# An encoder block on one core: the token tiles' transpositions a turn later, two weight splits behind the second chunk's numerators, and the last chunk and the last part's first token in another order

## The chip, the cores and the metric

The kernel runs on one core of one Trainium2 chip. The metric is the device time of one execution in microseconds (us). Before the change it is 2493.55, the median of three runs (2489.95 to 2499.76).

## The reference

Input `x` has 2048 tokens of 1024 values; one layer of an encoder is computed in fp32:

```python
xn = rmsnorm(x, norm_mix)
q, k, v, o, g = split(xn @ w_in)        # 4 heads, keys of 128, values of 256, gates g
h_fwd = mlstm_scan(q, k, v, g[0], g[1])                      # chunks of 128 tokens
h_bwd = flip(mlstm_scan(flip(q), flip(k), flip(v), g[2], g[3]))
h = head_norm(h_fwd + h_bwd) * sigmoid(o)
h1 = x + h @ w_out
h2 = h1 + square(relu(rmsnorm(h1, norm_mlp) @ w1)) @ w2      # 1024 -> 4096 -> 1024
gate = sigmoid(rmsnorm(h2, norm_ple) @ gate_w + gate_b)
out = rmsnorm(h2 + gate * (p @ ple_w), norm_final)           # p: 256 values per token
```

In each chunk the scan makes scores `q k^T`, weighs them with exponentials, multiplies them with `v` (the numerators), adds the carried state's share `q C`, divides by a denominator that comes out of the same product, and updates the state `C` for the next chunk.

## The kernel before, in words

Every large fp32 product is made of three matmuls: each operand is split into a high part (`hi`, a cast on ScalarE, ACT in the profile) and the remainder (`lo`, a subtraction on VectorE, DVE), and `mm3` multiplies hi·hi, hi·lo and lo·hi into one PSUM tile. Line 100 is the wrapper through which VectorE, ScalarE and TensorE instructions are recorded, so most rows of the profile carry it; the tile's name tells what a row is.

The program has four parts. First the input projections with the backward scan. Then the forward scan with the output projection, in 16 chunks (class `Chunk`, line 683), some 25 us each. Then the MLP, whose products are made by a seven-product scheme on 2x2 blocks (`run7`, line 1111) and whose down products end at about 2236 us. Then the last part (class `Tok`, line 1216): for 16 tiles of 128 tokens the gate product, the `ple_w` product and the last norm.

A chunk's steps are written as a list of short names that is walked for each turn of the loop over chunks (`step`, line 1375): `n0` and `n1` are the numerators with the forward and the backward state (PSUM tile `pn`, copied by ScalarE to `nt`), `s` the state product (`pu`, then `Cn` and its cast `Chi`), `T` the transpositions of the chunk before (`pth` out of `jk`, then `hThi` and `hTlo`), `S` the scores of the next chunk (`pS`), `e`, `k`, `w`, `q` and `v` its exponentials (`mb`), weighted keys (`wk`), weights (`pTh`), split queries (`qsh`) and split values (`vh`, `vl`), `p` the product of keys and gates of the chunk after next on GpSimd (`ib`, engine POOL), `m` and `me` the norm of the heads (root `rsa`, `rst`, `rsy`, then `jk`), `o0` and `o1` the two halves of the output projection of the chunk before (`pso`, added to the residual `xt`), and `d`, `d1`, `d2` loads. The Tile framework's scheduler takes this program order as priority and sets each engine's order from it, so that instructions of neighbouring steps end up interleaved.

There are three such lists beside the ordinary `ORDER`. `TR` (line 1390) is chunk 0, woven into the last input projections; in it `a0` to `a7` load and `c0` to `c7` split the eight tiles of `w_out` (`wst`, then `whi` and `wlo`). `ORDER_X` (line 1414) is used in turns that also prepare a tile of tokens for the MLP (`Tokens0.steps`, line 1009): `xl` loads 128 rows of the mixer's output (`raw`), `xn` norms them to `xs`, `xt` transposes them (eight matmuls into `pt`, copies to `zt`, one store). These steps begin in turn `XC` = 7 and run through turn 14. `TAIL` (line 1421) is the last chunk, mixed with the preparation of the first MLP product: `W` loads, `P1` and `P2` make its weight operands (`sa` and `op`), `Z`, `U` and `X` its token operands, `T15`, `y0` and `y1` are the last chunk's own transpositions and output projection.

Around the last part the dictionary `late` hangs loads and splits on the last steps of the down products; the two tiles of `ple_w` (`wpl`) are loaded in step 46 and split in step 47, the last. Then the loop over the 16 token tiles calls, for each, `tr0` of the next tile, `half(0)`, `tr1` of the next tile and `half(1)`, where `half` makes 24 matmuls into `pg`, six into `pl`, and the additions, sigmoid and squares behind them.

Of the kernel before, what the change touches and what calls it, by code (L numbers as in the profile page):

```python
# [17 lines left out]
S = 2048  # L18
# [17 lines left out]
def hybrid_mlstm_kernel(  # L36
# [28 lines left out]
    def ps_mm(name):  # L65
        return psm.tile([P, 512], F32, tag="mm", bufs=4, name=name)
# [1149 lines left out]
    class Tok:  # L1216
# [23 lines left out]

        def half(self, n):

            if n == 0:
                self.ss = small("ssf")
            sl = slice(n * 512, (n + 1) * 512)
            pg = ps_mm("pg")
            tk = slice((self.t % 4) * P, (self.t % 4 + 1) * P)
            for k in range(KD):
                mm3(pg, self.hi[:, k], self.lo[:, k], wgt[k].hi[:, sl], wgt[k].lo[:, sl], k == 0, k == KD - 1)
            pl = ps_tr("pl")  # L1250
            for k in range(2):
                mm3(pl, self.pt.hi[:, k, tk], self.pt.lo[:, k, tk], wpl[k].hi[:, sl], wpl[k].lo[:, sl], k == 0, k == 1)
            g, h = St("g", [P, 512]), self.h2[:, sl]
            V.tensor_tensor(g, pg, rowc["gb"][:, sl], op=ALU.add)
            act(g, g, AF.Sigmoid)
            V.tensor_tensor(g, pl, g, op=ALU.mult)
            V.tensor_tensor(h, g, h, op=ALU.add)
            A.activation(g, h, AF.Square, scale=1.0 / 32.0, accum_out=self.ss[:, n:n + 1])
# [116 lines left out]
    def step(c, nm):  # L1375
# [30 lines left out]
    def row_load(nm, src):  # L1406
        rowc[nm] = Ht(f"row_{nm}", [P, D])
        SP.dma_start(rowc[nm], src.partition_broadcast(P))


    XC = 7
    tp = {c: x0.steps(c - XC) for c in range(XC, XC + 8)}
    tp[XC][0] = lambda f=tp[XC][0]: (row_load("mlp", norm_mlp[0]), f())
    ORDER_X = "n0 d1 s e T S n1 d2 k w xl q sl m v d xn o0 o1 xt me p".split()
    for c in range(1, NC - 1):
        for nm in ORDER_X if c in tp else ORDER:
            if nm in ("xl", "xn", "xt"):
                tp[c][("xl", "xn", "xt").index(nm)]()
            else:
                step(c, nm)()  # L1420
    TAIL = "d2 W n1 Z1 Z3 T n0 Z2 Z4 o0 m me P1 X1 T15 P2 o1 U3 U1 y0 X2 U2 X3 y1".split()
    l = ch[NC - 1]
    u0 = up[0][0]
    extra = {"T15": l.transposes, "y0": lambda: l.out(0), "y1": lambda: l.out(1), "W": u0.left.dma,
             "P1": lambda: [f() for f in u0.prep[:3]], "P2": lambda: [f() for f in u0.prep[3:]],
# [44 lines left out]
    for g in range(4):  # L1470
# [6 lines left out]
            45: [wgt[5].prep, wgt[6].dma, wgt[7].dma, pp[0].get, toks[1].norm, toks[3].load],  # L1477
            46: [wgt[6].prep, wgt[7].prep, wpl[0].dma, wpl[1].dma, toks[0].tr0, pp[0].split],
            47: [wpl[0].prep, wpl[1].prep, toks[0].tr1, lambda: row_load("nf", norm_final)]}
    for s, fs in late.items():  # L1480
# [4 lines left out]
    for t in range(NC):  # L1485
        nx = toks[t + 1] if t + 1 < NC else None
        if nx:
            nx.tr0()
        toks[t].half(0)
        if t + 4 < NC:  # L1490
            toks[t + 4].load()
        if nx:
            nx.tr1()
        if t % 4 == 2 and t + 2 < NC:
            pp[t // 4 + 1].split()
        if t % 4 == 0 and t + 4 < NC:
            pp[t // 4 + 1].get()
        toks[t].half(1)
        if t > 0:
# [26 lines left out]
```

## Time and profile before

| | us |
|---|---|
| median of three runs | 2493.55 |
| profiled execution | 2496.48 |
| its span in the trace | 2494.8 |
| turn 1, from 600.32 to 630.05 | 29.73 |
| turn 4, from 679.44 to 702.74 | 23.30 |
| turn 7, from 751.85 to 778.02 | 26.17 |
| turns 8 to 14, from 778.02 to 937.20 | 159.18 |
| turn 15, from 937.20 to 955.90 | 18.70 |
| the last chunk's output projection, to 974.87 | 18.97 |

A turn is counted here from the first numerator matmul of a chunk to that of the next. It contains the end of one pass through the list and the beginning of another, since TensorE's order follows the scheduler. The last part starts at about 2236.5. In the timelines a row gives the start, the duration, the engine, the line, the operation with its output and inputs, how many of them are merged, and in brackets how long the engine had been idle and what released it.

### The profile page before, as it was taken

Reading aid. Unit: us, or ns where it says so; the run is one execution under the profiler, and the core shown is the slowest. Engines: PE = TensorE matmul, PEld = TensorE weight load, DVE = VectorE, ACT = ScalarE, POOL = GpSimd, SP = SyncE. Lnnn points to the kernel's source line nnn. Section 1 sums busy time; section 2 is a strip of 40 time slices with the busy share of each in tenths; the row PEclk is TensorE's granted clock in tenths of the full one; section 3 lists DMA queues with packets and bytes.
Section 4 is the critical chain, followed back from the end, with each engine's and each line's share of the span. In section 5 each row is a group of like instructions: output and inputs, shape, how many; then the busy total and the mean of one; then the engine's idle time right before and its main releaser. Section 6 shows DMA issues by size and latency. Waiting matters only on the chain.

```text
span 2494.8 us, 31616 instructions
## 1 busy us (share of the span) xinstructions
PE 2415.3 (97%) x11413; PEld 1987.1 (80%) x11413; DVE 1525.7 (61%) x2533; ACT 1134.5 (45%) x2134; POOL 610.9 (24%) x609
## 2 busy tenths in 40 slices
PE   7999999998899999999999999999999999999998
PEld 6988898787778887788878888787887888777776
DVE  5152336456787888656775445766676667655665
ACT  5031324336667885443353333444443444445554
POOL 1040022124433334344733333111111111110000
PEclk9999999999999999999999999999999999999999
DMA  7177337867566765455763331467686776882211
GB/s 250 48 207 238 91 101 243 271 216 276 201 210 212 254 234 190 144 169 169 257 203 125 114 112 59 160 146 178 142 185 166 176 173 153 184 219 84 85 54 49
DMA packets 270134, 420.72 MB, mean 169 GB/s; under 512 B 46441, under 2 KB 181993, under 8 KB 269977
## 3 DMA queue, kind: packets, MB, share of 16 engines
q1 hardware_dynamic: 211416, 299.03, 36.7%
q0 software_dynamic: 58272, 119.15, 20.4%
q8 instruction: 89, 1.46, 0.2%
q14 instruction: 69, 0.56, 0.1%
q10 hardware_dynamic: 288, 0.52, 0.1%
HBM read 253.43 MB, written 165.01 MB: 168 GB/s over the span
## 4 chain that ended last, share of the span: by engine, by line
PE 52%; DVE 4%; DMA 3%; ACT 2%; issue 1%; SPq 0%; POOL 0%; ACTq 0%; DVEq 0%
PE pa L100 26%; PE pb L100 13%; PE pc L100 6%; PE pg L100 5%; DMA hst<-hid_d 1%; PE pl L100 1%; DMA wst<-in_mlp_w 1%; DVE op L100 1%; PE pt L100 1%; DVE h L100 1%; DMA z<-tz_d 1%; ACT L100 1%; DVE xs L100 1%; PE pso L100 1%; DVE rst L100 1%
## 5 line engine op out<-in xcount | busy, mean ns | idle before, releaser
L100 PE MATMUL pa<-op 128*128 128x512 f32 x3072 | 753.2, 394 | 7.6 <-ACT e L100 4.1
L100 PEld LDWEIGHTS pa<-op 128*128 128x128 f32 x3072 | 575.4, 188 | 147.6 <-ACT e L100 7.8
L100 PE MATMUL pb<-op 128*128 128x512 f32 x1536 | 384.3, 394 | 1.2 <-DVE op L100 0.8
L100 PEld LDWEIGHTS pb<-op 128*128 128x128 f32 x1536 | 288.1, 188 | 70.0 <-ACT e L100 1.2
L100 PE MATMUL psf<-xT,whi 128*128 128x512 f32 x1024 | 320.8, 394 | 0.0
L100 DVE TENSOR_TENSOR op<-sa,op 128x768 fp32r<-128x768 f32 (+2 forms) x160 | 167.6, 1053 | 137.9 <-ACT op L100 106.1
L1162 POOL DMA_DIRECT2D h_d<-o x96 | 93.1, 977 | 567.8 <-DVE o L100 507.3
L100 PEld LDWEIGHTS psf<-xT,whi 128*128 128x128 f32 x1024 | 191.3, 188 | 43.7
L100 ACT COPY e<-pa 128x512 f32<-128x512 f32 x160 | 93.7, 586 | 261.6 <-PE pa L100 260.9
L100 ACT CAST op<-sa 128x768 fp32r<-128x768 f32 (+2 forms) x160 | 139.6, 879 | 146.7 <-PE pb L100 66.6
L100 PE MATMUL psf<-xT,wlo 128*128 128x512 f32 x512 | 201.8, 394 | 0.0
L100 PE MATMUL pc<-op 128*128 128x512 f32 x768 | 191.6, 394 | 0.2 <-DVE op L100 0.2
L100 PEld LDWEIGHTS pc<-op 128*128 128x128 f32 x768 | 144.1, 188 | 34.1 <-DVE op L100 0.6
L100 PE MATMUL psv<-whi,xT 128*128 128x272 f32 (+2 forms) x720 | 160.9, 317 | 0.6 <-DVE xT L98 0.6
L100 PEld LDWEIGHTS psv<-whi,xT 128*128 128x128 f32 x720 | 118.6, 188 | 9.8 <-DVE xT L98 0.8
L100 DVE TENSOR_TENSOR op<-wst,op 128x512 fp32r<-128x512 f32 x96 | 108.6, 1134 | 28.7 <-ACT op L100 16.0
L884 POOL TENSOR_TENSOR sa<-wst 128x512 f32<-128x512 f32 x32 | 60.4, 1887 | 263.9 <-PE pb L100 167.6
L100 ACT CAST op<-wst 128x512 fp32r<-128x512 f32 x96 | 79.3, 834 | 93.8 <-DVE op L100 59.3
L100 DVE TENSOR_TENSOR wlo<-wst,whi 128x1024 fp32r<-128x1024 f32 (+2 forms) x64 | 77.1, 1214 | 60.4 <-ACT whi L100 49.4
L100 PE MATMUL psv<-wlo,xT 128*128 128x272 f32 (+2 forms) x360 | 114.0, 317 | 0.0
L100 PEld LDWEIGHTS psf<-xT,wlo 128*128 128x128 f32 x512 | 96.1, 188 | 22.4
L100 PE MATMUL pg<-whi,xTl 128*128 128x512 f32 x256 | 102.5, 400 | 0.0
(228 smaller groups left out, 4318.6 us busy)
## 6 DMA issues: line engine op xcount, KB each, us to landing
wst<-in_mlp_w SPq DMA_DIRECT2D x96, 512.0 KB
h_d<-o POOLq DMA_DIRECT2D x96, 512.0 KB, 12.8
hid_d<-e SPq DMA_DIRECT2D x128, 256.0 KB
hst<-hid_d SPq DMA_DIRECT2D x64, 384.0 KB
wst<-in_mlstm_w_in SPq DMA_DIRECT2D x44, 512.0 KB
vst<-v_d SPq DMA_DIRECT2D x31, 512.0 KB
raw<-in_x SPq DMA_DIRECT2D x16, 512.0 KB
kq<-kq_d SPq DMA_DIRECT2D x16, 512.0 KB
```

Source lines behind the costliest of these rows:

```text
L100: r = f(*a, **kw)
L884: eng.tensor_tensor(s[:, 0], r1[:, :, P:], r2[:, :, P:], op=add_)
L1162: G.dma_start(rows(h1_d, 2 * q + i), o[i], accum_op=add_)
```

## The change

There are four edits.

`TR` loses `c6` and `c7`: the splits of the last two `w_out` tiles move into turn 1, behind `T` and behind `k w`, by a list `ORDER_1` of that turn's own.

`XC` becomes 6, so that token tiles are loaded and normed in turns 6 to 13, and `xt` in turn c now transposes the tile that was normed in turn c − 1, behind `n1`, where it stood at the turn's end for the same turn's tile. Transpositions are then in turns 7 to 14.

`TAIL` puts `P1`, `X1`, `o1` and `P2` ahead of the last chunk's transpositions, and its two output halves go behind the first of the seven products of the first MLP job (`u0.post[0]`).

In the last part `half` gives its gate product to a function `gate`. For the first token tile both gate products and both transpositions of the next tile are issued first, then the splits of the two `ple_w` tiles, then the rest of both halves. The `ple_w` loads move from step 46 to step 47.

```diff
-        def half(self, n):
+        def gate(self, n):
+            sl = slice(n * 512, (n + 1) * 512)
+            self.pg = pg = ps_mm("pg")
+            for k in range(KD):
+                mm3(pg, self.hi[:, k], self.lo[:, k], wgt[k].hi[:, sl], wgt[k].lo[:, sl], k == 0, k == KD - 1)
+
+        def half(self, n, gate=True):
...
+            if gate:
+                self.gate(n)
+            sl, pg = slice(n * 512, (n + 1) * 512), self.pg
...
         "D1 a0 D c0 o6a a1 o6b o7a v0 p0 S0 a2 o7b b0 c1 e0 d_ S k0 w0 a3 q0 b1 c2 p_ a4 n0 c3 e s d1 d2 sl k w a5 "
-        "n1 v b2 q m d c4 a6 me b3 c5 p c6 a7 c7").split()
+        "n1 v b2 q m d c4 a6 me b3 c5 p a7").split()
...
-    XC = 7
+    XC = 6
...
-    ORDER_X = "n0 d1 s e T S n1 d2 k w xl q sl m v d xn o0 o1 xt me p".split()
+    ORDER_1 = "n0 d1 s e T c6 S n1 d2 k w c7 q sl m v d o0 o1 me p".split()
+    ORDER_X = "n0 d1 s e T S n1 xt d2 k xl w q sl m v d xn o0 o1 me p".split()
...
-        for nm in ORDER_X if c in tp else ORDER:
+        for nm in ORDER_X if c in tp or c - 1 in tp else ORDER if c > 1 else ORDER_1:
...
-    TAIL = "d2 W n1 Z1 Z3 T n0 Z2 Z4 o0 m me P1 X1 T15 P2 o1 U3 U1 y0 X2 U2 X3 y1".split()
+    TAIL = "d2 W n1 Z1 Z3 T n0 Z2 Z4 o0 m me P1 X1 o1 P2 T15 U3 U1 X2 U2 X3".split()
...
+    u0.post[0][:0] = [lambda: l.out(0), lambda: l.out(1)]
...
-            46: [wgt[6].prep, wgt[7].prep, wpl[0].dma, wpl[1].dma, toks[0].tr0, pp[0].split],
-            47: [wpl[0].prep, wpl[1].prep, toks[0].tr1, lambda: row_load("nf", norm_final)]}
+            46: [wgt[6].prep, wgt[7].prep, toks[0].tr0, pp[0].split],
+            47: [wpl[0].dma, wpl[1].dma, toks[0].tr1, lambda: row_load("nf", norm_final)]}
...
-        toks[t].half(0)
+        if t == 0:
+            toks[t].gate(0)
+            pg0 = toks[t].pg
+            nx.tr1()
+            toks[t].gate(1)
+            pg1 = toks[t].pg
+            wpl[0].prep()
+            wpl[1].prep()
+            toks[t].pg = pg0
+        toks[t].half(0, t > 0)
```

ScalarE's order in turn 1, as one piece of the difference. `mb` are exponentials of the next chunk, `whi` casts of `w_out` tiles, `nt` the copies of numerators, `hThi` the high part of the transposed heads.

```order
 L100 ACTIVATE jk<-nt,rsy 128x256 x3
 L100 CAST whi<-wst 128x1024
-L100 ACTIVATE mb<-mb,gcol 128x128 x6
-L100 CAST whi<-wst 128x1024
-L100 ACTIVATE mb<-mb,gcol 128x128 x2
-L100 CAST whi<-wst 128x1024
+L100 ACTIVATE mb<-mb,gcol 128x128 x3
 L100 COPY nt<-pn 128x257 x4
-L100 CAST Chi<-Cn 128x1032
-L100 CAST hThi<-og 128x512 x2
+L100 ACTIVATE mb<-mb,gcol 128x128 x5
+L100 CAST Chi<-Cn 128x1032
```

Two casts have left the stretch ahead of the four `nt` copies; they stand behind `hThi` and behind the weights `pTh` now.

GpSimd's order in a turn with a token tile, before:

```order
L167 TENSOR_TENSOR qsl<-ib,qsh 128x1024
L641 MEMSET vh 128x4x2
L641 MEMSET vl 128x4x2
L642 MEMSET vh 128x4
L736 AFFINE_SELECT mb<-mb 128x512
L726 TENSOR_TENSOR ib<-kq,ib 128x512 x2
L706 DMA Chi<-cb_d 128x1032
L706 DMA Clo<-cb_d 128x1032
L736 AFFINE_SELECT mb<-mb 128x512
```

and after:

```order
L167 TENSOR_TENSOR qsl<-ib,qsh 128x1024
L641 MEMSET vh 128x4x2
L641 MEMSET vl 128x4x2
L642 MEMSET vh 128x4
L726 TENSOR_TENSOR ib<-kq,ib 128x512 x2
L706 DMA Chi<-cb_d 128x1032
L706 DMA Clo<-cb_d 128x1032
L736 AFFINE_SELECT mb<-mb 128x512 x2
```

Both products `ib` now stand ahead of both selects on `mb`, as they do in turns without a token tile.

ScalarE's order at the first token tile of the last part, before (`e` and `o` are the last results of the down products, `pTh` the high part of the tokens' `p`, `whi` the two `ple_w` tiles):

```order
L100 COPY e<-pb 128x512
L100 CAST xTh<-pt 128x512
L100 CAST pTh<-z 128x1024
L100 CAST whi<-wst 128x1024
L100 CAST xTh<-pt 128x512
L100 CAST whi<-wst 128x1024
L100 COPY o<-pa 128x512
L100 CAST xTh<-pt 128x512
```

and after:

```order
L100 CAST xTh<-pt 128x512
L100 COPY e<-pa 128x512
L100 COPY e<-pb 128x512
L100 CAST pTh<-z 128x1024
L100 CAST xTh<-pt 128x512 x2
L100 CAST whi<-wst 128x1024
L100 COPY o<-pa 128x512
L100 CAST whi<-wst 128x1024
```

Neither `ple_w` cast stands ahead of the two `xTh` casts any more.

## Rows read from the trace of the kernel before

**Rows 1.** The page's first part: busy time, share of the span and instructions of each engine (PEld is TensorE's weight load).

```profile
PE 2415.3 (97%) x11413; PEld 1987.1 (80%) x11413; DVE 1525.7 (61%) x2533; ACT 1134.5 (45%) x2134; POOL 610.9 (24%) x609
```

**Rows 2.** The waits of TensorE over the whole span: what waited for what, total us, times, the longest.

```profile
PE pu L100 <- ACT nt L100: 16.1, 14, 7.4
PE pt L100 <- DVE xs L100: 11.6, 16, 1.4
PE pt L100 <- DVE xTl L100: 5.8, 1, 5.8
PE pth L100 <- ACT jk L100: 3.3, 1, 3.3
```

**Rows 3.** Windows: from and to, length, busy us (instructions) of PE, PEld, DVE, ACT and POOL, granted clock of TensorE, share of the DMA engines, GB/s. In their order here: a low-clock stretch of turn 3, turn 4, turn 7, turns 8 to 14, turn 15, and the low-clock stretches of turn 1, of the last part, of the last chunk and of turn 7.

```profile
661.60:665.00 3.40, 3.39 (x16) 3.39 (x17) 3.37 (x8) 1.15 (x2) 0.42 (x1) 0.50 0.95 294
679.44:702.74 23.30, 21.52 (x126) 18.28 (x124) 17.70 (x35) 16.10 (x45) 8.65 (x11) 1.00 0.65 215
751.85:778.02 26.17, 23.78 (x125) 20.99 (x124) 18.95 (x36) 17.16 (x45) 8.43 (x10) 0.87 0.53 171
778.02:937.20 159.18, 149.92 (x925) 132.14 (x923) 133.38 (x286) 130.01 (x357) 60.09 (x68) 1.00 0.70 244
937.20:955.90 18.70, 17.62 (x101) 15.03 (x100) 12.47 (x24) 13.20 (x34) 5.22 (x3) 1.00 0.83 277
...
610.40:617.20 6.80, 4.72 (x22) 4.73 (x23) 3.31 (x7) 3.36 (x7) 0.00 (x0) 0.50 0.70 243
2238.50:2245.40 6.90, 3.10 (x10) 2.62 (x11) 2.74 (x3) 3.52 (x6) 0.17 (x1) 0.51 0.61 185
958.50:965.40 6.90, 5.43 (x16) 4.10 (x17) 5.41 (x8) 4.74 (x8) 0.28 (x1) 0.51 1.06 375
757.20:764.00 6.80, 6.37 (x29) 6.18 (x29) 3.44 (x8) 4.50 (x13) 2.34 (x4) 0.50 0.80 245
```

**Rows 4.** Timeline of turn 1, around the last cast of a `w_out` tile.

```profile
611.10 1.04 ACT L100 CAST whi<-wst 128x1024 fp32r<-128x1024 f32 x1 [3.92 <-DMA wst<-in_mlstm_w_out]
...
612.05 1.19 ACT L100 COPY nt<-pn 128x257 f32<-128x257 f32 x4
...
612.48 0.58 PE L100 MATMUL pu<-vh,wk 128*128 128x258 f32 x1 [7.38 <-ACT nt L100]
```

**Rows 5.** Timeline of the last chunk, on both sides of the end of chunk 14's output projection.

```profile
950.60 0.68 DVE L100 TENSOR_TENSOR xt<-pso,xt 128x512 f32<-128x512 f32 x1
950.60 1.30 POOL L884 TENSOR_TENSOR sa<-wst 128x512 f32<-128x512 f32 x1 [18.92 <-PE pso L100]
...
958.83 1.71 ACT L100 ACTIVATE jk<-nt,rsy 128x256 f32<-128x256 f32 x4 [4.56 <-DVE rsy L100]
959.39 1.97 PE L100 MATMUL pth<-ident,jk 128*128 128x128 f32 x8 [3.33 <-ACT jk L100]
...
961.94 0.79 PE L100 MATMUL pso<-whi,hThi 128*128 128x512 f32 x1 [0.58 <-ACT hThi L100]
```

**Rows 6.** Timeline of the last part's first token tile.

```profile
2239.34 1.04 ACT L100 CAST whi<-wst 128x1024 fp32r<-128x1024 f32 x1 [6.96 <-DMA wst<-in_ple_w]
...
2242.30 1.11 PE L100 MATMUL pt<-ident,xs 128*128 128x128 f32 x4 [5.76 <-DVE xTl L100]
...
2243.41 1.04 ACT L100 CAST whi<-wst 128x1024 fp32r<-128x1024 f32 x1 [2.54 <-DMA wst<-in_ple_w]
...
2244.49 1.23 DVE L100 TENSOR_TENSOR wlo<-wst,whi 128x1024 fp32r<-128x1024 f32 x1 [2.24 <-ACT whi L100]
...
2246.06 0.39 PE L100 MATMUL pg<-wlo,xTh 128*128 128x512 f32 x1
...
2246.29 0.39 PE L100 MATMUL pg<-whi,xTl 128*128 128x512 f32 x1
```

**Rows 7.** Timeline of turn 10, a turn with a token tile, which starts at 823.45.

```profile
825.91 1.09 PE L100 MATMUL pt<-ident,xs 128*128 128x128 f32 x8 [1.35 <-DVE xs L100]
826.32 2.53 POOL L726 TENSOR_TENSOR ib<-kq,ib 128x512 f32<-128x512 f32 x2
826.37 1.25 DVE L100 TENSOR_TENSOR rsy<-rsy,rst 128x4 f32<-128x4 f32 x1
...
828.77 0.28 PE L100 MATMUL pu<-vh,wk 128*128 128x258 f32 x1
...
838.22 0.32 SPq L696 DMA_DIRECT2D ib<-in_d  x1
```

**Rows 8.** Timeline of turn 4, a turn without a token tile, which starts at 679.44, from the end of the turn before it on.

```profile
677.12 3.59 POOL L726 TENSOR_TENSOR ib<-kq,ib 128x512 f32<-128x512 f32 x2 [1.75 <-DMA ib<-in_d]
677.23 1.23 DVE L100 TENSOR_SCALAR rsa<-ssh 128x4 f32<-128x4 f32 x1
...
679.50 1.24 DVE L100 TENSOR_TENSOR rst<-rsa,rsy 128x4 f32<-128x4 f32 x1
680.77 0.16 DVE L100 TENSOR_TENSOR rst<-rst,rsy 128x4 f32<-128x4 f32 x1
...
681.37 1.71 ACT L100 ACTIVATE jk<-nt,rsy 128x256 f32<-128x256 f32 x4 [2.44 <-DVE rsy L100]
...
684.26 0.39 PE L100 MATMUL pu<-vh,wk 128*128 128x258 f32 x1 [1.28 <-ACT nt L100]
```

**Rows 9.** Timeline of VectorE at the start of turn 2.

```profile
628.97 2.34 DVE L100 TENSOR_TENSOR vl<-vst,vh 128x1024 fp32r<-128x1024 f32 x1 [0.77 <-ACT vh L100]
```

More of the change, by code (lines that the diff above doesn't have):

```diff
@@ L1239, in hybrid_mlstm_kernel @@
         tr0, tr1 = (lambda self: self.tr(0)), (lambda self: self.tr(1))
-        def half(self, n):
+        def gate(self, n):
[4 more added lines that the diff above has]
+        def half(self, n, gate=True):
             if n == 0:
                 self.ss = small("ssf")
-            sl = slice(n * 512, (n + 1) * 512)
-            pg = ps_mm("pg")
+            if gate:
+                self.gate(n)
+            sl, pg = slice(n * 512, (n + 1) * 512), self.pg
             tk = slice((self.t % 4) * P, (self.t % 4 + 1) * P)
-            for k in range(KD):
-                mm3(pg, self.hi[:, k], self.lo[:, k], wgt[k].hi[:, sl], wgt[k].lo[:, sl], k == 0, k == KD - 1)
             pl = ps_tr("pl")
@@ L1408, in row_load @@
         SP.dma_start(rowc[nm], src.partition_broadcast(P))
-    XC = 7
+    XC = 6
     tp = {c: x0.steps(c - XC) for c in range(XC, XC + 8)}
     tp[XC][0] = lambda f=tp[XC][0]: (row_load("mlp", norm_mlp[0]), f())
-    ORDER_X = "n0 d1 s e T S n1 d2 k w xl q sl m v d xn o0 o1 xt me p".split()
+    ORDER_1 = "n0 d1 s e T c6 S n1 d2 k w c7 q sl m v d o0 o1 me p".split()
+    ORDER_X = "n0 d1 s e T S n1 xt d2 k xl w q sl m v d xn o0 o1 me p".split()
     for c in range(1, NC - 1):
-        for nm in ORDER_X if c in tp else ORDER:
-            if nm in ("xl", "xn", "xt"):
-                tp[c][("xl", "xn", "xt").index(nm)]()
+        for nm in ORDER_X if c in tp or c - 1 in tp else ORDER if c > 1 else ORDER_1:
+            if nm == "xt":
+                tp.get(c - 1, [lambda: None] * 3)[2]()
+            elif nm in ("xl", "xn"):
+                tp.get(c, [lambda: None] * 3)[("xl", "xn").index(nm)]()
+            elif nm in ("c6", "c7"):
+                wo[int(nm[1])].prep()
             else:
                 step(c, nm)()
-    TAIL = "d2 W n1 Z1 Z3 T n0 Z2 Z4 o0 m me P1 X1 T15 P2 o1 U3 U1 y0 X2 U2 X3 y1".split()
+    TAIL = "d2 W n1 Z1 Z3 T n0 Z2 Z4 o0 m me P1 X1 o1 P2 T15 U3 U1 X2 U2 X3".split()
     l = ch[NC - 1]
     u0 = up[0][0]
-    extra = {"T15": l.transposes, "y0": lambda: l.out(0), "y1": lambda: l.out(1), "W": u0.left.dma,
+    extra = {"T15": l.transposes, "W": u0.left.dma,
              "P1": lambda: [f() for f in u0.prep[:3]], "P2": lambda: [f() for f in u0.prep[3:]],
@@ L1488, in hybrid_mlstm_kernel @@
             nx.tr0()
-        toks[t].half(0)
+        if t == 0:
[8 more added lines that the diff above has]
+        toks[t].half(0, t > 0)
         if t + 4 < NC:
             toks[t + 4].load()
-        if nx:
+        if nx and t > 0:
             nx.tr1()
@@ L1497, in hybrid_mlstm_kernel @@
             pp[t // 4 + 1].get()
-        toks[t].half(1)
+        if t == 0:
+            toks[t].pg = pg1
+        toks[t].half(1, t > 0)
         if t > 0:
```

## The prediction, before any run of the changed kernel

> **What bounds the kernel now.** I read the busy shares first, then the waits of TensorE, then the windows around the places the diff touches, then their timelines. TensorE is busy for 97% of the span and VectorE, the next, for 61% [rows 1], so time can come only from its idle stretches and from the stretches in which it ran at its lower clock. The list of its waits names the idle ones [rows 2]: 16.1 us before a state product (`pu`) for the copy of a numerator (`nt`), 7.4 of them in one wait; 11.6 us in 16 waits of a token's transposition (`pt`) for its normalized tile (`xs`); one wait of 5.8 for the low half of a transposed token (`xTl`); one of 3.3 for the normalized heads (`jk`). The windows give the clock as granted [rows 3]: 1.00 (2.4 GHz) over turns 8 to 14, 0.50 (1.2 GHz) in short stretches, three of which hold a place the diff edits. A matmul that runs in such a stretch takes twice as long, so half of TensorE's busy time there is lost. I call a chunk's stretch between two starts of its first numerators a turn.
>
> The kernel's own sum is made against the profiled execution, 2496.48 us; the median of the runs shown, 2493.55, is 2.93 lower, and I subtract that at the end. A difference under 0.5% (12.5 us) is about what a measurement of this kernel can't tell from no change.
>
> **Turn 1: the last two w_out splits.** Before, ScalarE stands 3.92 us before the second of the two casts, for a weight's transfer that lands at 611.10, and only then copies four numerators, for which TensorE waits 7.38 us [rows 4]. The low clock holds from 610.40 to 617.20 with 4.72 us of TensorE work in it [rows 3], half of it lost: 2.36. Together 9.7. The changed order puts both casts behind the copies, so this wait goes. What is late next: the four copies with the six or eight small `mb` activations before them, some 1.0 us before `pu`; the `out` product, whose heads come from ScalarE next to a cast of 1.04, some 1.7; the low half of the last tile, some 0.6. 9.7 − 3.3 = 6.4, of which I take **−6.2**, from −8.5 (only the 1.0 is left) to −4 (the low clock stays). These three left-over waits are estimates from the durations in [rows 4].
>
> **Last chunk.** TensorE waits 3.33 us for `jk` and 0.58 for `hThi` [rows 5], and from 958.50 the clock is 0.50 with 5.43 us of work in it, half lost: 2.7 [rows 3]. That is 6.6. Now the first MLP product's twelve matmuls (2.8 us at the full clock) and the numerators' second half are put in front of the transpositions. They cover most of the 3.33, but ScalarE has the casts of that product to do ahead of `jk`, so `jk`, 1.71 long, comes later too; I leave 1.4 for it and 0.9 for `hThi`, whose successor no longer has filler. 6.6 − 2.3 = **−4.3**, from −6 to −2.5.
>
> **First token of the last part.** ScalarE waits 6.96 us for the first of two `ple_w` tiles, in front of the cast that makes `xTh`; so the transposed token is late and TensorE waits 5.76 [rows 6]. The low clock from 2238.50 holds 3.10 us of work, 1.55 lost [rows 3]: 7.3 together. In the changed program the gate products of both halves, 48 matmuls of 0.23 (the step between two of them) [rows 6], with both transpositions, stand ahead of the first use of `ple_w`, which puts that use at about 2247.2. The second tile landed at 2243.41; its cast and subtraction, 1.04 and 1.23 [rows 6], are done by 2245.8. So 1.4 us of cover is left if the transfers, now issued one step later, land as before; landing over 1.4 later, each further us is a us of wait. I take **−6.2**, from −7.3 to −4.5.
>
> **Turns 8 to 14: the transposition.** These take 159.18 us, 22.74 each, with 149.92 of TensorE work, 21.42 each, at clock 1.00 [rows 3]. Of the idle 1.32 a turn nearly all is the transposition's wait for `xs` (1.35 in turn 10 [rows 7]). A turn later that wait goes, since `xs` is then a turn old. But it was not only lost: while TensorE stood there and did the eight transpositions (1.09), ScalarE caught up, and `pu` came with no wait at 828.77 [rows 7]. Without transposition in that place `pu` follows the numerators directly, as in the turns without token work. Turn 4 is the nearest row: 23.30 long with 21.52 of work [rows 3], 1.78 idle, most of it the 1.28 before `pu` [rows 8]. There `jk` (1.71) must pass before the `nt` copies, and `jk` waits 2.44 for the reciprocal root (`rsa`, `rst`, `rsy`: small operations of VectorE).
>
> Why that root is late, the rows show: GpSimd's two `ib` products run from 677.12 for 3.59, and the VectorE operations that start just behind the beginning of one take 1.23 and 1.24 in place of 0.16 [rows 8]. In the changed order of token turns GpSimd's products come before both selects of `mb`, as in turn 4, so they meet the root's operations, unless their data come later or earlier. In turn 10 one such operation met them too (1.25), but behind the wait, where it cost little [rows 7]. The data of `ib` are asked for at 838.22, in the turn before [rows 7], and now behind the token's store in SyncE's queue, so they land about when the turn begins. I take turn 4's 1.78, and 0.3 more for the token's own small operations, which share the two engines: 21.42 + 1.78 + 0.3 = 23.5, so 0.75 a turn and 5.3 over seven. No row shows the changed order; the idle share lies between 0.9 (the wait at `pu` alone, smaller than in turn 4) and 3.3 (the case of the rival below), that is −3 to +14 over seven turns.
>
> With waits of this size TensorE fell to 0.50 in turns 2 to 7: 3.40 us from 661.60 and 6.80 from 757.20 [rows 3], 5.1 us lost in six turns; in turns 8 to 14 it never did. I take two stretches of 3.4 there, 1.7 each: 3.4 us, from 0 to 12 (one in each turn). Sum: **+8.7**, bounds −6 (the first rival below) and +25 (the second).
>
> VectorE's addition of the residual (`xt`) now stands between the root's steps in its queue. In the trace it took 0.68 while a GpSimd operation of 1.30 began at the same time [rows 5], so I cost it at nothing beyond its place. The Trainium skill (SBUF — State Buffer, section Who interferes with whom) says that a VectorE instruction with at most one input in SBUF, outside the two-port modes, does not contend with GpSimd; the other input of `xt` is in PSUM, and this row agrees.
>
> **Turns 2 to 7 and turn 15.** Before, the eight transpositions stand in turns 8 to 15, after, in turns 7 to 14. Turn 7 took 26.17, with 6.37 us of work at clock 0.50 from 757.20 [rows 3], 3.2 lost. It now takes over a transposition (about 1 us) and becomes a turn like those above: 23.5 without the low clock, 27 with it; I take 25.2, **−1**, from −3 to +1. Turn 15, 18.70 with 17.62 of work [rows 3], gives up its transposition and the wait before it: 17.0, **−1.7**, from −2.2 to +1. Turns 2 to 6 keep their order, but that a token's load and norm join turn 6; I give 0, within 2.
>
> **The sum.** −6.2 − 4.3 − 6.2 + 8.7 − 1 − 1.7 = −10.7. 2496.48 − 10.7 = 2485.8, less 2.93: **2482.9**. With the terms' smaller bounds the forecast alone reaches from 2475 to 2492.
>
> **Rivals.**
> No collision: the `ib` products are done before the root begins, or start after it. Then `pu` waits less than 1.35 and the token turns gain. Of the idle 1.32 a turn I give back 0.85: 7 × 0.85 = 6, and turn 7 comes out at its lower bound, −3. −6.2 − 4.3 − 6.2 − 6 − 3 − 1.7 = −27.4, or 2496.48 − 27.4 − 2.93: **2466**. For it: in turn 10 the products met only the root's last step [rows 7], with a GpSimd order that differs by one select. Against it: turn 4, whose order is the one now copied [rows 8].
>
> GpSimd first, on the slower side: if an `ib` product starts ahead of the long subtraction `vl`, that takes 2.34 [rows 9], where one of the same width takes 1.23 without [rows 6], so the root and `jk` come 1.1 later each turn: 23.5 + 1.1 = 24.6, 1.86 over 22.74, 13.0 in seven turns; and with waits of 3 us the low clock comes each turn, 11.9 more. −19.4 + 24.9 = +5.5: **2499**. It decides against the change once a token turn loses over 19.4 / 7 = 2.8, that is from 25.5 a turn. For it: turn 2, where it happened. Against it: turns 8 to 14 showed no low clock at all. The Trainium skill, in the same section, says that the shared pair is an exclusive lock and that issue order decides who blocks; the 2.34 and the 1.23 to 1.25 agree with that.
>
> The ends don't hold: the `ple_w` tiles land some 4 us later than before, since they are asked for a step later, and the last chunk's `jk` slips as far as its filler reaches. Then these two give half of their 10.5: −10.7 + 5.3: **2488**. This is also the case in which the change doesn't do what it says: the stalls are moved, not removed.
>
> **How the numbers follow.** The forecast 0.52, no collision 0.22, GpSimd first 0.15, ends that don't hold 0.11. The range reaches from the first rival, 2466, to 2497, short of the full price of the second. Faster by over 0.5% means under 2481.1: all of the first rival (0.22) and a little over four tenths of the forecast (0.22): 0.44. Slower means over 2506: the second rival with its bounds: 0.04. The rest, 0.52, is within 0.5%.
>
> **What would show it.** In the changed profile: no wait over 2 us before `pu` in turn 1; the wait for `xTl` in the last part gone, and the second `ple_w` cast done before the first `pl`; the wait of `pth` for `jk` under 1.5; no waits of `pt` for `xs` in turns 7 to 14, but waits of `pu` for `nt` of 1 to 2.5 in each, with small VectorE operations of 1.2 in the root beside `ib`. If these last are missing and the turns take 22 or less, the first rival is right; if `vl` takes 2.3 and the clock falls in most token turns, the second. What would make the prediction wrong altogether is a stall in a place where I see none, in turns 2 to 6 above all, whose code the diff leaves alone but whose pools and transfers it shifts.

## The result and the profile after

The changed kernel takes 2475.81 us, the median of four runs (2474.46 to 2477.36), beside 2493.72 for four runs of the kernel before: a ratio of 0.9926, 95% interval 0.9905 to 0.9947. That is 17.9 us less, where 10.6 less was forecast; it lies in the range and on the faster side of 0.5%, the case given 0.44. The two profiled executions stand 22.0 us apart (2496.48 and 2474.46), since the one of before was slower than its median by 2.8 and the one after faster than its own by 1.4.

The windows of the changed kernel, with the columns of [rows 3]: turn 1, turns 2 to 6, turn 7, turns 8 to 14, turn 15, the stretch from the end of chunk 14's output projection to the first `pc` product, and two of its low-clock stretches. (`pa`, `pb` and `pc` are PSUM tiles of the MLP's products, `op` their operands.)

```profile
599.36:622.45 23.09, 20.88 (x126) 18.18 (x124) 20.40 (x33) 19.52 (x47) 9.97 (x11) 1.00 0.87 317
622.45:744.14 121.69, 110.38 (x621) 94.17 (x620) 93.48 (x172) 82.59 (x227) 46.11 (x50) 0.97 0.58 197
744.14:768.17 24.03, 22.16 (x134) 18.93 (x132) 19.47 (x43) 18.68 (x52) 8.77 (x10) 1.00 0.73 242
768.17:930.70 162.53, 154.38 (x925) 135.52 (x924) 140.25 (x279) 129.45 (x357) 58.14 (x68) 0.98 0.73 245
930.70:947.07 16.37, 16.37 (x93) 14.24 (x92) 12.69 (x22) 11.87 (x30) 5.15 (x4) 1.00 1.02 360
947.07:963.26 16.19, 15.11 (x69) 12.12 (x68) 16.10 (x20) 8.38 (x12) 2.54 (x1) 1.00 0.55 168
...
817.70:821.10 3.40, 3.40 (x18) 3.40 (x18) 3.01 (x8) 2.68 (x8) 1.27 (x2) 0.50 0.93 329
889.40:892.80 3.40, 3.26 (x15) 3.27 (x16) 2.55 (x6) 3.40 (x9) 0.63 (x1) 0.50 0.95 369
```

Put beside the trace of before, cut at the same instructions of TensorE (in the kernel before, turn 15 begins with the token's transposition, so there its start is the end of the output projection ahead of it):

| stretch | before, us | after, us | change | forecast |
|---|---|---|---|---|
| start to turn 1 | 600.32 | 599.36 | −1.0 | 0 |
| turn 1 | 29.73 | 23.09 | −6.6 | −6.2 |
| turns 2 to 6 | 121.80 | 121.69 | −0.1 | 0 |
| turn 7 | 26.17 | 24.03 | −2.1 | −1 |
| turns 8 to 14 | 159.18 | 162.53 | +3.4 | +8.7 |
| turn 15 | 18.70 | 16.37 | −2.3 | −1.7 |
| to the first `pc` | 21.60 | 16.19 | −5.4 | −4.3 |
| to the end of the down products | 1257.88 | 1258.78 | +0.9 | 0 |
| last part, to TensorE's last | 248.12 | 239.38 | −8.7 | −6.2 |
| sum | | | −22.1 | −10.7 |

Every term that was forecast came out with its sign. Half of the miss of 11 is in turns 8 to 14. The +0.9 and the −8.7 of the last two stretches belong together: four `pg` matmuls of 0.23 of the first token now run before the down products end, so that edit is worth −7.8.

TensorE's waits after, with the columns of [rows 2]:

```profile
PE pu L100 <- ACT nt L100: 10.5, 18, 1.3
...
PE pth L100 <- ACT jk L100: 3.7, 4, 1.0
...
PE pu L100 <- DVE Cn L100: 2.2, 1, 2.2
...
PE pso L100 <- ACT nt L100: 1.4, 1, 1.4
...
PE pt L100 <- DVE xs L100: 1.0, 6, 0.2
```

Against [rows 2], the 7.4 in front of `pu`, the 5.8 for `xTl` and the 3.3 for `jk` in one piece are gone, and so are the eight waits of some 1.3 for `xs`. New are three waits of 0.9 of `pth` for `jk` in turns 10 to 12, one of 1.0 in turn 7, and 2.2 of `pu` for `Cn` in turn 13.

Turn 1 answers to [rows 4]; here are its first `pu`, the cast of the last tile but one and the first `pso` matmul, from the timelines of ScalarE and TensorE.

```profile
609.86 1.04 ACT L100 CAST whi<-wst 128x1024 fp32r<-128x1024 f32 x1
```

```profile
604.13 0.38 PE L100 MATMUL pu<-vh,wk 128*128 128x258 f32 x1 [0.65 <-ACT nt L100]
...
611.22 0.50 PE L100 MATMUL pso<-whi,hThi 128*128 128x512 f32 x1 [1.36 <-ACT nt L100]
```

`pu` waits 0.65 in place of 7.38, `pso` 1.36 behind the moved cast: the two left-over waits stand where they were put at 1.0 and 1.7, and no stretch at 0.50 is left in this turn.

The last part answers to [rows 6].

```profile
2225.86 1.05 ACT L100 CAST whi<-wst 128x1024 fp32r<-128x1024 f32 x1 [4.82 <-DMA wst<-in_ple_w]
...
2226.77 0.60 PE L100 MATMUL pt<-ident,xs 128*128 128x128 f32 x4
...
2228.92 1.05 ACT L100 CAST whi<-wst 128x1024 fp32r<-128x1024 f32 x1 [1.53 <-DMA wst<-in_ple_w]
...
2230.00 1.23 DVE L100 TENSOR_TENSOR wlo<-wst,whi 128x1024 fp32r<-128x1024 f32 x1 [1.84 <-ACT whi L100]
...
2233.26 0.39 PE L100 MATMUL pl<-whi,pTh 128*128 128x512 f32 x1
```

ScalarE still waits for both `ple_w` tiles, 4.82 and 1.53, but no longer ahead of a cast that the transpositions wait for: `pt` follows the gate products without a wait. The second tile's low half is done at 2231.23, and its first use is at 2233.26: 2.0 us of cover, where 1.4 were counted.

What decides turns 8 to 14 is seen by laying two of them side by side. First turn 8, which starts at 768.17 and takes 21.22; VectorE, GpSimd and ScalarE.

```profile
768.98 0.22 DVE L100 TENSOR_TENSOR rst<-rsa,rsy 128x1 f32<-128x1 f32 x2
769.16 0.23 DVE L100 TENSOR_TENSOR rst<-rst,rsy 128x1 f32<-128x1 f32 x2
```

```profile
769.67 3.54 POOL L726 TENSOR_TENSOR ib<-kq,ib 128x512 f32<-128x512 f32 x2 [5.76 <-DVE rst L100]
```

```profile
769.85 1.70 ACT L100 ACTIVATE jk<-nt,rsy 128x256 f32<-128x256 f32 x4
```

Then turn 10, which starts at 811.33 and takes 25.18; the same engines, and TensorE.

```profile
812.29 1.45 DVE L100 TENSOR_TENSOR rst<-rsa,rsy 128x1 f32<-128x1 f32 x2
813.66 1.33 DVE L100 TENSOR_TENSOR rst<-rst,rsy 128x1 f32<-128x1 f32 x2
```

```profile
812.42 2.54 POOL L726 TENSOR_TENSOR ib<-kq,ib 128x512 f32<-128x512 f32 x2 [4.80 <-DVE xt L100]
```

```profile
815.42 1.71 ACT L100 ACTIVATE jk<-nt,rsy 128x256 f32<-128x256 f32 x4 [1.77 <-DVE rsy L100]
```

```profile
815.99 0.73 PE L100 MATMUL pth<-ident,jk 128*128 128x128 f32 x3 [0.88 <-ACT jk L100]
817.44 0.40 PE L100 MATMUL pu<-vh,wk 128*128 128x258 f32 x1 [0.72 <-ACT nt L100]
```

In turn 8 the two `ib` products start 1.50 us into the turn, when the root is nearly done: its pairs of small operations take 0.22 and 0.23, and `jk` starts 1.68 in. In turn 10 the products start at 1.09, the same pairs take 1.45 and 1.33, `jk` starts 4.09 in, TensorE waits 0.88 and 0.72, and the clock falls to 0.50 from 817.70 (3.40 us, 1.7 lost). Over the turns, taken from the timelines (us from the turn's start; the landing is the last of the 16 updates of that load's semaphore in the trace):

| turn | 8 | 9 | 10 | 11 | 12 | 13 | 14 |
|---|---|---|---|---|---|---|---|
| landing of the `ib` load | 1.34 | 1.92 | 0.97 | 0.82 | 0.71 | 0.61 | 1.29 |
| first `ib` product | 1.50 | 2.09 | 1.09 | 0.98 | 0.88 | 0.83 | 1.45 |
| `jk` | 1.68 | 2.41 | 4.09 | 3.77 | 3.72 | 6.07 | 2.79 |
| length | 21.22 | 21.94 | 25.18 | 23.45 | 23.09 | 25.12 | 22.53 |

So the forecast's collision is in turns 10 to 13, the first rival in turns 8 and 9, and turn 14 lies between. In turn 13 `jk` is later still because `xs` (1.28) stands ahead of the root's last operation in VectorE's order. The `ib` loads are asked for 6.3 to 6.95 us ahead of the turn in all seven, and the product starts 7.6 to 8.4 behind that. The bracket of the timeline names a small VectorE operation as what GpSimd waited for; the semaphores that the product waits for say otherwise: in six of the seven turns it starts 0.12 to 0.17 us behind the landing of its own load, and in turn 13 0.21 behind it, where GpSimd was just done issuing another load. In the kernel before, the first product of turns 8 to 14 started 3.3 to 6.4 us behind its landing, since it stood behind the first select. So with the products ahead of the selects it is the landing, some tenths of a us earlier or later, that decides whether they meet the root.

### The profile page after: what moved, and what is told of

Read it like the earlier page. It is cut to its first block, busy times and chain, and to the rows that moved or that the text cites. A ratio compares the mean times of both kernels' runs of the same rounds, so it can differ in the third digit from the quotient of the medians.

```text
span 2472.8 us, 31645 instructions
## 1 busy us (share of the span) xinstructions
PE 2410.8 (97%) x11413; PEld 1981.7 (80%) x11413; DVE 1530.2 (62%) x2533; ACT 1134.8 (46%) x2134; POOL 603.4 (24%) x609
## 3 DMA queue, kind: packets, MB, share of 16 engines
q8 instruction: 89, 1.46, 0.2%
## 4 chain that ended last, share of the span: by engine, by line
PE 69%; issue 11%; DVE 8%; ACT 6%; DMA 4%; POOL 2%; SPq 0%; ACTq 0%; DVEq 0%; POOLq 0%
PE pa L100 27%; PE pb L100 13%; PE pc L100 7%; PE pg L100 6%; PE psf L100 5%; PE psv L100 3%; PE pso L100 2%; ACT jk L100 1%; PE pn L100 1%; PE pl L100 1%; PE pu L100 1%; DVE rst L100 1%; DVE nt L100 1%; PE pt L100 1%; DMA hst<-hid_d 1%
## 5 line engine op out<-in xcount | busy, mean ns | idle before, releaser
L100 PEld LDWEIGHTS psf<-xT,wlo 128*128 128x128 f32 x512 | 96.1, 188 | 22.4
L100 PE MATMUL pso<-whi,hThi 128*128 128x512 f32 x256 | 101.6, 398 | 2.4 <-ACT nt L100 1.4
```

Source lines behind the costliest of these rows:

```text
L100: r = f(*a, **kw)
```

## The experiments

The theory: the four edits add up, and the token turns are set by whether the `ib` products run beside the root. Rivals: an edit's gain hangs on another edit; the removed wait for `xs` is a gain, and the collision costs nothing.

**Each edit alone.** Four kernels, each the kernel before with one edit of the diff: `only_w` the two `w_out` splits in turn 1, `only_x` the token tiles, `only_tail` the last chunk, `only_last` the last part.

```diff
only_w
-        "n1 v b2 q m d c4 a6 me b3 c5 p c6 a7 c7").split()
+        "n1 v b2 q m d c4 a6 me b3 c5 p a7").split()
+    ORDER_1 = "n0 d1 s e T c6 S n1 d2 k w c7 q sl m v d o0 o1 me p".split()
only_x
-    XC = 7
+    XC = 6
-    ORDER_X = "n0 d1 s e T S n1 d2 k w xl q sl m v d xn o0 o1 xt me p".split()
+    ORDER_X = "n0 d1 s e T S n1 xt d2 k xl w q sl m v d xn o0 o1 me p".split()
only_tail
-    TAIL = "d2 W n1 Z1 Z3 T n0 Z2 Z4 o0 m me P1 X1 T15 P2 o1 U3 U1 y0 X2 U2 X3 y1".split()
+    TAIL = "d2 W n1 Z1 Z3 T n0 Z2 Z4 o0 m me P1 X1 o1 P2 T15 U3 U1 X2 U2 X3".split()
+    u0.post[0][:0] = [lambda: l.out(0), lambda: l.out(1)]
only_last
-        toks[t].half(0)
+        if t == 0:
+            toks[t].gate(0)
...
+            wpl[1].prep()
```

> Only the two w_out splits move into turn 1; all else as before. If the parts add up: turn 1 falls from 29.7 to about 23.1 us as it did with all four edits, nothing else moves, and the time is 6.6 us under the kernel before (about 0.27%). Rival, that part of turn 1's gain came from the low clock falling elsewhere by chance: turn 1 still has a stretch at 0.50 and the gain is 4 us or less.

> Only the token tiles' transposition moves a turn later, with load and norm a turn earlier. If the collision of the two ib products with the head norm's root sets the token turns: turns in which an ib product starts 0.8 to 1.3 us into the turn take 23 to 25 us, turns in which it starts 1.5 us in or later take 21 to 22.5; turns 8 to 14 together 157 to 164 us (159.2 before), and the whole within 5 us of the kernel before. Rival, that the removed wait for xs is a clean gain: turns 8 to 14 at 150 to 153 us and the whole 10 us faster.

> Only the last chunk's order changes. If the parts add up: from the start of the last chunk's wait to the first pc product 16.2 us in place of 21.6, the whole 5.4 us faster. Rival, that the filler only moves the wait (forecast's rival): half of that, 2.7 us.

> Only the first token tile of the last part changes. If the parts add up: the 5.8 us wait for xTl and the low clock behind it go, 7 to 9 us faster; no pl waits for ple_w. Rival, that the ple_w tiles land late: a wait of pl for wlo of 2 us or more, gain of 5 us or less.

| kernel | ratio to before | interval |
|---|---|---|
| `only_w` | 0.9973 | 0.9962 to 0.9984 |
| `only_x` | 0.9988 | 0.9979 to 0.9997 |
| `only_tail` | 0.9991 | 0.9982 to 1.0001 |
| `only_last` | 0.9963 | 0.9949 to 0.9976 |

By the ratios these are −6.7, −3.0, −2.2 and −9.2 us, and they sum to −21.1, beside −18.5 for the whole (0.9926). With intervals of 2.2 to 3.4 us to either side of each, the times don't tell whether the edits add up. `only_w` and `only_last` came as expected: in the trace of the first, turn 1 is 23.1 long, in that of the other the last part is 239.2 (from 248.1).

`only_x` has the collision as in the changed kernel: its turns 8 to 14 take 163.0 us. One that starts its `ib` products at 1.86 takes 21.4, one that starts them at 0.74 takes 23.5. A turn at 1.40, between the two ranges that were given, still collided (24.0), while in `after_again` one at 1.26 took 22.4 and one at 1.46 took 23.6: the bound is not sharp.

`only_tail` missed: its time (−2.2, interval −4.5 to +0.2) rules out 5.4 but not the rival's 2.7; by its trace the stretch that was edited is 0.5 us shorter, neither of the two. The timeline of TensorE says why.

```profile
957.32 0.69 PE L100 MATMUL pth<-ident,jk 128*128 128x128 f32 x2 [3.30 <-ACT jk L100]
957.66 0.78 PE L100 MATMUL pa<-op 128*128 128x512 f32 x1
```

The scheduler put two of the transpositions ahead of the filler, so the wait for `jk` stayed, at 3.30 as in [rows 5]. In the changed kernel the same list gives another order, with all twelve `pa` in front; here TensorE's and ScalarE's rows there.

```profile
948.43 1.71 ACT L100 ACTIVATE jk<-nt,rsy 128x256 f32<-128x256 f32 x4 [0.28 <-DVE rsy L100]
```

```profile
947.07 2.95 PE L100 MATMUL pa<-op 128*128 128x512 f32 x12
949.86 1.03 PE L100 MATMUL pth<-ident,jk 128*128 128x128 f32 x8
951.98 0.50 PE L100 MATMUL pso<-whi,hThi 128*128 128x512 f32 x1 [1.08 <-ACT hThi L100]
```

**The changed kernel without one edit.** `no_x` takes the token tiles' edit back, `no_tail` the last chunk's; `after_again` is the changed kernel, on the chip of `no_x`.

```diff
no_x, against the changed kernel
-    XC = 6
+    XC = 7
-    ORDER_X = "n0 d1 s e T S n1 xt d2 k xl w q sl m v d xn o0 o1 me p".split()
+    ORDER_X = "n0 d1 s e T S n1 d2 k w xl q sl m v d xn o0 o1 xt me p".split()
no_tail, against the changed kernel
-    TAIL = "d2 W n1 Z1 Z3 T n0 Z2 Z4 o0 m me P1 X1 o1 P2 T15 U3 U1 X2 U2 X3".split()
+    TAIL = "d2 W n1 Z1 Z3 T n0 Z2 Z4 o0 m me P1 X1 T15 P2 o1 U3 U1 y0 X2 U2 X3 y1".split()
-    u0.post[0][:0] = [lambda: l.out(0), lambda: l.out(1)]
```

> The changed kernel unedited, on the chip of the other three runs: about 0.9926 of the kernel before, some 18 us faster. Turns 8 to 14 between 157 and 164 us, long turns those in which an ib product starts 0.8 to 1.3 us into the turn.

> The changed kernel without the token tiles' edit (XC 7 and the old ORDER_X), the other three edits in. If the edits add up only in part, because the last chunk's head norm is early only when turn 15 has no transposition: turns 8 to 14 at 159 us again (3 less than changed), turn 7 at 25 to 26 (2 more), turn 15 at 18.7 (2.3 more), and the last chunk's wait of pth for jk back at 3.3 (4 more): 3 to 6 us over the changed kernel. Rival, that the token tiles' edit only cost its 3 us in turns 8 to 14: 2 to 4 us under the changed kernel.

> The changed kernel with the old TAIL (and the output halves back in it). If most of the gain at the end of the scan came from the token tiles' edit (jk earlier since turn 15 has no transposition): the wait of pth for jk is 1.5 us as in only_x, from the end of chunk 14's output projection to the first pc product 17.8 us in place of 16.2 to 17.3, and the whole 0.5 to 2 us over the changed kernel. Rival, that the order of the last chunk earns its 5 us by itself: a wait of 3.3 us for jk and 5 us over the changed kernel.

`after_again` 0.9925 (0.9912 to 0.9937), `no_x` 0.9930 (0.9918 to 0.9942), `no_tail` 0.9924 (0.9905 to 0.9942): by time none can be told from the changed kernel, so neither the 3 to 6 us over it expected of `no_x` nor the 0.5 to 2 of `no_tail` shows in the medians (2478.59, 2476.88 and 2476.97 for `after_again`). The traces tell them apart. The wait of `pth` for `jk` over the whole span, total, times and longest, in `no_x`, then in `no_tail`:

```profile
PE pth L100 <- ACT jk L100: 3.3, 1, 3.3
```

```profile
PE pth L100 <- ACT jk L100: 6.2, 6, 1.5
```

In `no_x` turns 8 to 14 take 159.25 again, as expected, and the wait of 3.33 is back with the new list in place, and with it the order of `only_tail`, transpositions first; in `no_tail`, with the old list, the one in the last chunk is 1.49, as in `only_x` (1.46). So the wait shrinks by 1.9 us by the token tiles' edit: chunk 15's head norm comes out earlier once turn 15 has no transposition and no wait for `xs`. From the end of chunk 14's output projection to the first `pc` it takes 21.6 before, 17.9 in `only_x` and in `no_tail`, 16.2 and 17.3 in the two profiles of the changed kernel: 3.7 for the token tiles' edit, 0.6 to 1.7 for the list behind it. With the list and without the token tiles' edit it is 21.1 in `only_tail`, where the clock is at 0.50 for 6.8 us, and 19.9 in `no_x`, where it is for 3.4.

**The collision taken away.** `late_ib` is the changed kernel with the products of a chunk issued a turn later and behind that chunk's selects on GpSimd, which come some 5 us into the turn. The ordinary list and that of turn 1 are edited in the same way as the list shown.

```diff
+                    with tc.issue_after(self.sel.ins):
+                        G.tensor_tensor(self.ib[:, d], self.kq[:, 1], self.ib[:, d], op=ALU.mult)
...
-                G.affine_select(out=self.mb[:, d], in_=self.mb[:, d], pattern=[[0, H], [sgn, P]],
+                self.sel = G.affine_select(out=self.mb[:, d], in_=self.mb[:, d], pattern=[[0, H], [sgn, P]],
...
-    ORDER_X = "n0 d1 s e T S n1 xt d2 k xl w q sl m v d xn o0 o1 me p".split()
+    ORDER_X = "n0 d1 s e p T S n1 xt d2 k xl w q sl m v d xn o0 o1 me".split()
```

> The changed kernel with GpSimd's two ib products put behind both selects of the turn, so that they can't run beside the root (rsa, rst, rsy) of the chunk before. If their collision with the root sets jk and with it the wait of pu: no small VectorE operation of the root over 0.5 us, jk starts 1.6 to 2.5 us into every turn, turns 8 to 14 at 21.2 to 22 us each (148 to 154 in all, 162.5 before this edit), turns 2 to 6 at 21.9 to 23 in place of 24.3, and the whole 12 to 20 us under the changed kernel. Rival, that the products cost as much wherever they lie, since they then meet Cn, og and the low halves: new waits of pso or pn for VectorE, turns 8 to 14 over 158 and the whole within 5 us of the changed kernel.

It takes 2457.37 us, 0.9842 of before (0.9829 to 0.9856), where `after_again` beside it took 2476.97: 19.6 us less than the changed kernel. Its windows: turns 2 to 6, and turns 8 to 14.

```profile
620.71:735.81 115.10, 107.45 (x621) 91.22 (x620) 87.80 (x171) 81.34 (x226) 39.89 (x49) 1.00 0.62 209
...
759.22:907.91 148.69, 148.64 (x925) 132.13 (x924) 132.03 (x279) 128.01 (x355) 59.40 (x68) 1.00 0.79 266
```

And the rows of VectorE, ScalarE and GpSimd in its turn 11, which starts at 823.20:

```profile
824.01 0.22 DVE L100 TENSOR_TENSOR rst<-rsa,rsy 128x1 f32<-128x1 f32 x2
824.19 0.23 DVE L100 TENSOR_TENSOR rst<-rst,rsy 128x1 f32<-128x1 f32 x2
```

```profile
824.87 1.70 ACT L100 ACTIVATE jk<-nt,rsy 128x256 f32<-128x256 f32 x4
```

```profile
830.53 2.53 DVE L100 TENSOR_TENSOR hTlo<-og,hThi 128x512 fp32r<-128x512 f32 x2
```

```profile
829.51 3.00 POOL L730 TENSOR_TENSOR ib<-kq,ib 128x512 f32<-128x512 f32 x2
```

Turns 8 to 14 take 21.24 each and hold 0.05 us of idle TensorE in all seven; turns 2 to 6 took 121.7 and take 115.1, with the clock at 1.00. From turn 1 on to the MLP the clock is not at 0.50 once. The rival, that the products cost as much elsewhere, falls for this place: in turn 11 they run beside `og`, `mb` and `hTlo`, and the pair of `hTlo` takes 2.53 in place of some 1.3 (0.68 each in the changed kernel), but TensorE does not wait for it.

`late_no_x` is `late_ib` with the token tiles' edit taken back in the way of `no_x`.

```diff
-    XC = 6
+    XC = 7
-    ORDER_X = "n0 d1 s e p T S n1 xt d2 k xl w q sl m v d xn o0 o1 me".split()
+    ORDER_X = "n0 d1 s e p T S n1 d2 k w xl q sl m v d xn o0 o1 xt me".split()
```

> The kernel of late_ib (ib products behind the selects) with the token tiles' edit taken back (XC 7, the old ORDER_X). If the removed wait for xs is worth its full 1.3 us a turn once no product meets the root: turns 8 to 14 at 22.7 again (159 in all, against 149 in late_ib), turn 15 some 2 us longer, the last chunk's wait for jk back at some 3 us, and the whole 13 to 18 us over late_ib. Rival, that the edit is worth little even without the collision: within 6 us of late_ib.

2472.24 us, 0.9898 (0.9883 to 0.9913), 14.9 over `late_ib` in medians taken beside two groups of runs of before (2496.22 and 2496.85). The expected 13 to 18 came, and the last chunk's wait for `jk` is back at 3.29. Its windows over turns 2 to 6 and turns 8 to 14:

```profile
627.45:742.54 115.09, 107.43 (x622) 91.22 (x620) 87.98 (x172) 81.00 (x227) 40.92 (x49) 1.00 0.64 213
765.78:925.24 159.46, 149.73 (x925) 132.18 (x923) 126.15 (x287) 129.70 (x359) 60.38 (x68) 1.00 0.71 243
```

Turns 2 to 6 are those of `late_ib`, turns 8 to 14 those of before (159.18): without the collision the token tiles' edit takes 10.8 us off these seven turns, where with it, it added 3.4. The later products in turn are worth some 8 us without that edit (0.9930 for `no_x`, 0.9898 here), and 19.6 with it.

`early_ib` goes the other way: the loads for the products are asked for earlier in each turn, in all three lists.

```diff
-    ORDER_X = "n0 d1 s e T S n1 xt d2 k xl w q sl m v d xn o0 o1 me p".split()
+    ORDER_X = "n0 d1 s e T S n1 d xt d2 k xl w q sl m v xn o0 o1 me p".split()
```

> The changed kernel with the loads of kq, mb and ib of the chunk after next asked for right behind n1, early in the turn, so that the ib products can run long before the root. Same theory by another way: where both products are done before vl begins, turns of 21.2 to 22 us; where one still starts beside vl or the root, 23 to 25. The scheduler puts one of the two products back behind the selects in some turns, so less than late_ib: 5 to 15 us under the changed kernel. Rival: no turn gets shorter, since the wait of pu is set by the nt copies alone.

2475.79 us, 0.9914 (0.9900 to 0.9929): not told apart from the changed kernel, so the expected 5 to 15 us missed. In its trace turns 8 to 14 take 161.4 us, and no operation of the root takes over 0.6 in them, but over the span TensorE now waits for other things:

```profile
PE pn L100 <- DVE vl L100: 9.0, 9, 1.3
PE pn L100 <- POOL vh L642: 7.2, 5, 2.3
```

Seven of the nine waits for `vl` are in turns 8 to 14, one in each, of 0.67 to 1.27; all five for `vh` lie ahead of them. The values' own load is not what makes `vl` late: VectorE goes from other work to `vl` without a pause. That work is the root's collision in another place, as this row from ahead of turn 9 shows (`Clo` is the low part of the state).

```profile
783.25 3.44 DVE L100 TENSOR_TENSOR Clo<-Cn,Chi 128x1032 fp32r<-128x1032 f32 x1
```

Ahead of each of the seven waits `Clo`, which is ahead of `vl` in VectorE's order, starts beside a GpSimd product (`ib`, or `qsl` of the split queries) and takes 2.32 to 3.44 us; in the changed kernel it takes 1.23. So by the trace the collision only moved, to operations that TensorE waits for as well.

**The last part's two halves.** `splits_only` is the kernel before with the `ple_w` splits alone moved; `loads_46` is the changed kernel with the loads back in step 46.

```diff
splits_only, against before
-            47: [wpl[0].prep, wpl[1].prep, toks[0].tr1, lambda: row_load("nf", norm_final)]}
+            47: [toks[0].tr1, lambda: row_load("nf", norm_final)]}
...
+        if t == 0:
+            wpl[0].prep()
+            wpl[1].prep()
loads_46, against the changed kernel
-            46: [wgt[6].prep, wgt[7].prep, toks[0].tr0, pp[0].split],
-            47: [wpl[0].dma, wpl[1].dma, toks[0].tr1, lambda: row_load("nf", norm_final)]}
+            46: [wgt[6].prep, wgt[7].prep, wpl[0].dma, wpl[1].dma, toks[0].tr0, pp[0].split],
+            47: [toks[0].tr1, lambda: row_load("nf", norm_final)]}
```

> The kernel before with only the splits of the two ple_w tiles moved behind the first token's transposition (behind tr0 of the second tile), the gate products in their old order and the loads in step 46. If the edit of the last part needs both of its halves: the wait for xTl goes, but the first pl comes at about 2242 and waits some 3 us for the low half of the second ple_w tile, done at 2245.7; the last part 3 to 5 us shorter, where the whole edit gave 9. Rival, that the splits alone held the xTl cast: the whole 9 us.

> The changed kernel with the two ple_w loads back in step 46. If the tiles land in time either way, as the forecast's 1.4 us of cover has it: no wait of pl in either, the last part 239.4 us as before, the whole within the noise of the changed kernel. Rival, that the later load keeps SyncE's queue or the staging buffers free for others: other waits in the last part, 2 us or more.

One run each, 2492.53 and 2479.83 us, is too few to rank; the traces decide. In `splits_only` the wait for `xTl` is gone and `pl` waits instead:

```profile
2242.80 0.50 PE L100 MATMUL pl<-whi,pTh 128*128 128x512 f32 x1 [1.79 <-ACT whi L100]
2244.06 0.50 PE L100 MATMUL pl<-wlo,pTh 128*128 128x512 f32 x1 [0.76 <-DVE wlo L100]
```

That is 2.55 us and a stretch at 0.50 from 2244.5, 3.4 long; the last part takes 245.3, 2.8 less than before (3 to 5 were expected), where the whole edit takes 8.7 off. Both the splits and the order of the gate products are needed. In `loads_46` no `pl` waits, as in the changed kernel, so the later load cost nothing. Its last part takes 240.8, not the 239.4 expected, but the four `pg` matmuls (0.9) that the changed kernel makes ahead of it are in it there.

## Why the prediction was right, and where its sizes were off

**Turn 1** was right in mechanism and size (−6.6, forecast −6.2); `only_w` gives it by itself.

**The last part** was right in mechanism; of its term, −7.8 in place of −6.2, the deduction from 7.3 for a late landing was not needed, since 2.0 us of cover was left, and a wait of `pa` for the last down result (0.44 in the trace of before) went too.

**The last chunk** was right in sum (−5.4, forecast −4.3) by luck, and wrong in its reason. The step that failed is "They cover most of the 3.33": by itself the new list left the wait of 3.3 as it was, since the scheduler put transpositions ahead of the filler, and most of the gain (3.7 of it) came from chunk 15's norm being earlier, by the token tiles' edit, which the prediction had priced in turn 15 only.

**Turns 8 to 14** carry the largest error: +3.4 against +8.7. The step that failed is taking turn 4's idle time for all seven ("so 0.75 a turn and 5.3 over seven"). The collision was there and cost what was said where it happened: turns 10 to 13 take 24.2 in the mean, or 23.4 without what the low clock cost in two of them, where 23.5 was forecast. The waits had another form: in turns 10 to 12 first `pth` waited for `jk` (0.9), which the prediction does not name for these turns, and then `pu` for `nt` (0.3 to 1.0); in turn 13 `pu` waited for `Cn`. But whether it happened hung on some 0.5 us in the start of the `ib` products, and their loads, said to land "about when the turn begins", landed 0.6 to 1.9 us into it.

Two low-clock stretches of 3.4 were taken, and two came, which is partly luck: the other four profiles of this order have two, one, none and none in these turns (`only_x`, `after_again`, `no_tail`, `loads_46`). They give 163.0, 159.6, 160.2 and 160.4 for turns 8 to 14: +2 in the mean of the five.

The prediction's account of such stretches in turns 2 to 7 of the kernel before also misses a third, in turn 5, so that 6.8 and not 5.1 us were lost there:

```profile
709.40:712.80 3.40, 3.26 (x15) 2.83 (x15) 2.09 (x6) 1.24 (x5) 1.70 (x3) 0.50 0.99 290
```

**The first rival** held in turns 8 and 9, and `late_ib` shows its price: not 0.85 a turn but 1.50 (22.74 to 21.24). **The second rival** did not show in the token turns: `vl` took 1.22 or 1.23 in all seven. In turns 5 and 6, whose order is as before, it took 2.26 and 1.94 with `ib` in front of it, and these two turns took 25.2 and 23.9. The Trainium skill's page SBUF — State Buffer (section Who interferes with whom), cited for the exclusive pair and the issue order, agrees with both: the small operations that start behind an `ib` product ran until that product's end (1.45 and 1.33 for the two pairs), those that start ahead of it kept their 0.22 a pair.

Of the rest, turn 7 and turn 15 came 1.1 and 0.6 beyond forecast, and 1.0 fell in a stretch no edit touches. All the sizes erred to the same side, towards a smaller gain.

## What to carry to other kernels

A wait in front of TensorE can be time in which a second engine catches up; before it is filled, price what the engine behind it will then be late with. Where GpSimd and VectorE share a turn, put a long GpSimd operation by an explicit order behind the short chain of VectorE operations that others wait for: that was worth 19.6 us here, as much as the four edits together (19.9 on the same chip), though only some 8 without the token tiles' edit. It matters which operations it meets there: in `early_ib` they were others that TensorE waits for, and nothing was gained. And run each edit of a bundle alone and take each away: most of what the last chunk's list seemed to give came from another edit, and the same list became another order once its neighbours differed.

## What was not expected of the hardware

A turn of 22 us hangs on half a microsecond: with the first `ib` product at 1.50 us the turn took 21.2, at 1.09 it took 25.2, 1.7 of which was the clock at 0.50 for 3.40 us. The clock fell there behind two waits of TensorE, 0.88 and 0.72 us with 0.73 us of work between. But it stayed at 1.00 in the next turn of the same profile, behind longer ones with less work between:

```profile
840.85 0.44 PE L100 MATMUL pth<-ident,jk 128*128 128x128 f32 x2 [0.93 <-ACT jk L100]
842.30 0.39 PE L100 MATMUL pu<-vh,wk 128*128 128x258 f32 x1 [1.01 <-ACT nt L100]
```

It also stayed at 1.00 in turn 10 of `after_again` and of `no_tail`, behind 0.82 and 0.73 and behind 0.84 and 0.73, and in turns 8 to 14 of `late_no_x`, where TensorE stood 1.3 to 1.4 once in each. So the waits alone do not tell when it falls, and what does is open.
